# Both operand sums of a weight pair made together: gate/up by seven products in a two-layer decoder trunk

## The chip, the cores and the metric

The kernel runs on one core of one Trainium2 chip. The metric is the device time of that core in microseconds (us). Before the change three timed runs gave 2051.58, 2051.83 and 2052.47 us, a median of 2051.83 us. One further execution was taken by the profiler; every duration below comes from it. TensorE is called PE, VectorE DVE, ScalarE ACT, GpSimd POOL; SP is the engine that issues most of the weight loads.

## The reference

Two layers; each is a half-step feed-forward block (FFN), a mixer (a gated linear recurrence beside a sliding-window attention, both behind one wide projection) and a second half-step FFN. Width D = 1024, 512 tokens, inner FFN width 2816, everything in float32.

```
def swiglu(h, w_gate, w_up, w_down):
    return (jax.nn.silu(h @ w_gate) * (h @ w_up)) @ w_down

for l in range(DEPTH):
    h = rms_norm(x, gn[0])
    x = x + 0.5 * rms_norm(swiglu(h, w_ffn1_gate[l], w_ffn1_up[l], w_ffn1_down[l]), gn[1])
    h = rms_norm(x, gn[2])
    ...
    mixed = jax.nn.sigmoid(gate_a) * y_hg + jax.nn.sigmoid(gate_b) * y_at
    x = x + rms_norm(mixed @ w_out[l], gn[3])
    h = rms_norm(x, gn[4])
    x = x + 0.5 * rms_norm(swiglu(h, w_ffn2_gate[l], w_ffn2_up[l], w_ffn2_down[l]), gn[5])
```

## The kernel before

**Two halves of every operand.** Each float32 operand of a matmul is split into a high half (a cast, by ACT) and a low half (value minus high half), and a product is three matmuls: high by high, high by low, low by high (`mm3`). The weights stream from memory in units of 128x1024 float32 (`w32`, four buffers, loaded by SP at L244 and L247), and each unit is split into `whi` and `wlo` (six buffers of each). L359 is the cast to `whi` on ACT. The low half is made in one of two ways: by a subtraction on DVE (L363), or by writing the negated value on ACT (L355) and letting a POOL-issued DMA add the weight to it in memory (L358).

**Seven products.** Most gate and up columns are not computed as two plain products. A block of 128 gate columns, 128 up columns and the two halves of the 1024 input rows form a 2x2 block product that is computed with seven half-size products instead of eight (`sevenths`). For the weights this takes four operands per pair of units, the items a, b, c and d: a is the first unit `w`, d the second half of the second unit `v`, b is a tile `tt` of two sums of `w` and `v` (L340, L341), and c a second tile `tt` of two more sums, which start from b's first sum. a and d get their low halves through POOL's DMA, b and c through DVE's L363. One pair is 7 x 4 x 3 = 84 matmuls of 128x256. PE uses the pair in the order a (products 1 and 2), b (5 and 7), c (6 and 4), d (3).

**Loops.** `fast` runs such pairs: 15 of them in the first FFN and 19 in each of the three others, 72 together. The mixers' branch gates take 4 more pairs in each layer (`gates`), each followed by 24 matmuls of 128x512. So there are 80 pairs. Each loop starts with one short extra matmul of 144 columns (`lead`). After a `fast` loop comes `down`, which begins with three plain stretches (`both`) and then further seven-product work for the down projection, whose operands (`Late`) DVE, ACT and POOL make from the gated results.

**What a pair asks of DVE besides.** After the products of pair k DVE combines the PSUM results with L1063, L1065, L1069 and L1070, ACT applies the Silu (L1084), and DVE multiplies gate by up (L1087), the gated product.

**What sets the order.** Only PE follows the program as it is written. For the other engines a scheduler chooses, but instructions that go through `pin` (or `hold`, while `tight` is set in `fast`) keep the written order among themselves. `ahead` decides when the next item is split: up to four items ahead of the one that PE is using in `fast`, and no more than six items in flight. So item b of pair k+2 is split (and writes over the buffers of item d of pair k) while PE is in pair k+1, and c of pair k+2 when a of pair k+1 is free. The gated product is held back as `gate` and put out at a chosen place by `product()`, here within the split of b.

In numbers of the profile, b's and c's lines before the change are L340, L341 (sums of b), L359 and L363 (its halves), L347, L348 (sums of c), L359 and L363 again. A `tt` tile has two buffers.

Of the kernel before, what the change touches and what calls it, by code (L numbers as in the profile page):

```python
# [7 lines left out]
F32 = mybir.dt.float32  # L8
# [3 lines left out]
ALU = mybir.AluOpType  # L12
# [3 lines left out]
P = 128  # L16
D = 1024
# [29 lines left out]
def trunk(ctx: ExitStack, tc: tile.TileContext, xin, wall, gains, lbT, hgain, sinks, c_dist, c_mask, c_ident, out):  # L47
    nc = tc.nc
    cp = ctx.enter_context(tc.tile_pool(name="cp", bufs=1))
    sb = ctx.enter_context(tc.tile_pool(name="sb", bufs=1))  # L50
# [9 lines left out]
    def nm(s):  # L60
        seq[0] += 1
        return f"{s}_{seq[0]}"
# [85 lines left out]
    pin = tc.keep_in_program_order  # L148
# [10 lines left out]
    class Stream:  # L159
# [164 lines left out]
        def split(self):  # L324
            it = self.items[self.done]
            if it.kind[0] == "p":
                return self.quarter(it)
            u, last = it.u, it.kind in "uvd"
            self.load(u + (1 if it.kind in "uv" else 2))
            it.hi, it.lo = (sb.tile([P, D + 64], F32R, tag=t, name=nm(t), bufs=WS)[:, it.at : it.at + D] for t in ("whi", "wlo"))  # L330
            w, h = self.raw[u], (slice(0, D // 2), slice(D // 2, D))
            cols = (slice(0, D),)
            if it.kind == "u" and u < 2:
                cols = h
            if it.kind in "bcd":
                v = self.raw[u + 1]
            if it.kind == "b":

                self.t13 = sb.tile([P, D], F32, tag="tt", name=nm("tt"), bufs=2)
                pin(nc.vector.tensor_tensor(self.t13[:, h[0]], w[:, h[0]], v[:, h[0]], op=ALU.add))  # L340
                pin(nc.vector.tensor_tensor(self.t13[:, h[1]], v[:, h[0]], v[:, h[1]], op=ALU.add))  # L341
                w = self.t13
                self.product()
            elif it.kind == "c":

                t = sb.tile([P, D], F32, tag="tt", name=nm("tt"), bufs=2)
                pin(nc.vector.tensor_tensor(t[:, h[0]], self.t13[:, h[0]], v[:, h[1]], op=ALU.add))  # L347
                pin(nc.vector.tensor_tensor(t[:, h[1]], t[:, h[0]], w[:, h[1]], op=ALU.add))  # L348
                w = t
            elif it.kind == "d":  # L350
                w = v
                cols = h[1:]
            for c in cols:
                if it.kind in "vad":
                    i = nc.scalar.mul(it.lo[:, c], w[:, c], -1.0)  # L355
                    if self.pinned or self.tight:
                        pin(i)
                    nc.gpsimd.dma_start(it.lo[:, c].bitcast(F32), w[:, c], accum_op=ALU.add)  # L358
                i = nc.scalar.copy(it.hi[:, c], w[:, c])  # L359
                if u < 6 or self.pinned or self.tight:  # L360
                    pin(i)
                if it.kind not in "vad":
                    self.hold(nc.vector.tensor_tensor(it.lo[:, c], w[:, c], it.hi[:, c].bitcast(F32), op=ALU.subtract))  # L363
            self.done += 1
            self.flight += 1
            if last:
                nu = u + (1 if it.kind in "uv" else 2)
                for i in range(u, nu):
                    self.raw.pop(i)
                    self.freed += 1  # L370
                self.load(self.freed + W32)
# [128 lines left out]
    def pair_split(v, how=split):  # L500
        return how(v, to=(big(F32R, [P, 2, S // 2]), big(F32R, [P, 2, S // 2])))
# [13 lines left out]
    class First(Quarters):  # L515
# [44 lines left out]
        def sums(self):  # L560

            k = len(self.x56)
            a = []
            for i in range(2):
                f = xs[k + 4 * i]
                nc.vector.scalar_tensor_tensor(f, f, g_sb[:, 0, 0, k + 4 * i : k + 4 * i + 1], self.rb, op0=ALU.mult, op1=ALU.mult)
                a.append([f[:, c] for c in HALF])
            self.x124.append([])
            for v in (a[0][0], a[1][0], a[1][1]):
                x = big(F32R, [P, 2, S // 2])  # L570
                split(v, to=(x[:, 0, :], x[:, 1, :]))
                self.x124[k].append(x)
            for x, v in zip((self.x56, self.x37), quarter_sums(a[0][0], a[1][0], a[0][1], a[1][1])):
                x.append(pair_split(v))
# [74 lines left out]
    class Late:  # L649
# [20 lines left out]
        def first(self, k):  # L670
            x = big(F32R, [P, 2, S // 2])
            self.x1.append(split(self.src[k][:, HALF[0]], to=(x[:, 0, :], x[:, 1, :]), hold=pin))
# [979 lines left out]
```

## Time and profile before

| | |
|---|---|
| timed runs | 2051.58, 2051.83, 2052.47 us |
| the profiled execution, span | 2051.3 us |
| PE clock granted, mean | 0.999 |
| ACT's cast of a `tt` tile (L359, 128x1024) | 160 of 1051 ns (median) |
| DVE's low half of a `tt` tile (L363, 128x1024) | 160 of 1226 ns |
| a sum of 128x512 on DVE (L340, L341, L347, L348) | 80 each, 681 to 692 ns |
| ACT waiting for L348 before L359 | 192.3 us in 75 waits |
| DVE waiting for L359 before a `tt` tile's L363 | 129.1 us in 146 waits |

The span runs from the first to the last instruction of the profiled execution; the median of the timed runs is 0.5 us longer. Durations include a tail in which the next instruction of the same engine already runs: a matmul of 128x256 is listed with 0.28 us and the next one starts 0.113 us later, and a DVE instruction listed with 0.69 us is followed by the next after about 0.60. So lengths of stages are read from start to start. Idle time of an engine that nobody waits for costs nothing.

### The profile page before, as it was taken

Reading aid. Unit: us, or ns where it says so; the run is one execution under the profiler, and the core shown is the slowest. Engines: PE = TensorE matmul, PEld = TensorE weight load, DVE = VectorE, ACT = ScalarE, POOL = GpSimd, SP = SyncE. Lnnn points to the kernel's source line nnn. Section 1 sums busy time; section 2 is a strip of 40 time slices with the busy share of each in tenths; the row PEclk is TensorE's granted clock in tenths of the full one; section 3 lists DMA queues with packets and bytes.
Section 4 is the critical chain, followed back from the end, with each engine's and each line's share of the span. In section 5 each row is a group of like instructions: output and inputs, shape, how many; then the busy total and the mean of one; then the engine's idle time right before and its main releaser. Section 6 shows DMA issues by size and latency. Waiting matters only on the chain. (4 is left out here: it accounts for less than half of the span.)

```text
span 2051.3 us, 36423 instructions
## 1 busy us (share of the span) xinstructions
PE 2032.0 (99%) x13553; PEld 1815.3 (88%) x13553; DVE 1623.7 (79%) x2894; ACT 1249.4 (61%) x2213; POOL 268.3 (13%) x318
## 2 busy tenths in 40 slices
PE   9999999999999999999999999999999999999998
PEld 8899878877888999997899998888778989999987
DVE  5887889767676778888988878987686858788888
ACT  7556687446355556657866566874554545665684
POOL 0111140000000011113201111400000100111140
PEclk9999999999999999999999999999999999999999
DMA  8577788312237357778757778872122553777694
GB/s 257 152 194 186 189 187 238 117 65 70 73 94 215 113 146 192 190 188 205 200 157 191 193 186 203 179 230 92 62 73 62 137 194 102 182 190 194 175 201 123
DMA packets 166801, 328.07 MB, mean 160 GB/s; under 512 B 19072, under 2 KB 85088, under 8 KB 166624
## 3 DMA queue, kind: packets, MB, share of 16 engines
q1 hardware_dynamic: 122416, 228.16, 33.5%
q0 software_dynamic: 44064, 97.54, 27.3%
q8 instruction: 106, 1.74, 0.4%
q14 instruction: 71, 0.58, 0.1%
q10 hardware_dynamic: 144, 0.05, 0.0%
HBM read 213.43 MB, written 14.73 MB: 111 GB/s over the span
## 5 line engine op out<-in xcount | busy, mean ns | idle before, releaser
L116 PE MATMUL acc<-s,whi 128*128 128x256 f32 (+1 forms) x4998 | 1023.7, 304 | 0.3 <-ACT whi L359 0.3
L116 PEld LDWEIGHTS acc<-s,whi 128*128 128x128 f32 x4998 | 793.6, 188 | 47.0 <-issue 3.2
L116 PE MATMUL acc<-s,wlo 128*128 128x256 f32 (+1 forms) x2488 | 755.3, 304 | 5.3 <-DMA wlo<-w 5.2
L116 PEld LDWEIGHTS acc<-s,wlo 128*128 128x128 f32 x2488 | 467.9, 188 | 30.6 <-DMA wlo<-w 7.4
L116 PE MATMUL acc<-whi,s 128*128 128x512 f32 x1360 | 443.9, 394 | 4.9 <-ACT whi L288 3.6
L359 ACT CAST whi<-w 128x1024 fp32r<-128x1024 f32 (+1 forms) x310 | 284.8, 926 | 144.9 <-PE acc L116 103.5
L359 ACT CAST whi<-tt 128x1024 fp32r<-128x1024 f32 x160 | 168.1, 1051 | 250.5 <-DVE tt L348 192.3
L358 POOL DMA_DIRECT2D wlo<-w x178 | 154.7, 870 | 1232.8 <-ACT wlo L355 987.0
L116 PEld LDWEIGHTS acc<-whi,s 128*128 128x128 f32 x1360 | 255.8, 188 | 64.3 <-ACT whi L288 4.8
L363 DVE TENSOR_TENSOR wlo<-tt,whi 128x1024 fp32r<-128x1024 f32 x160 | 196.1, 1225 | 131.4 <-ACT whi L359 129.1
L116 PE MATMUL acc<-wlo,s 128*128 128x512 f32 x680 | 267.3, 393 | 1.8 <-DVE wlo L296 1.6
L116 PE MATMUL aux<-s,whi 128*128 128x256 f32 (+1 forms) x1296 | 228.5, 279 | 0.0
L363 DVE TENSOR_TENSOR wlo<-w,whi 128x1024 fp32r<-128x1024 f32 (+1 forms) x132 | 157.4, 1206 | 74.2 <-ACT whi L359 73.9
L116 PEld LDWEIGHTS aux<-s,whi 128*128 128x128 f32 x1296 | 196.6, 188 | 1.1 <-issue 0.5
L116 PE MATMUL aux<-s,wlo 128*128 128x256 f32 (+1 forms) x648 | 180.4, 278 | 0.0
L116 PEld LDWEIGHTS acc<-wlo,s 128*128 128x128 f32 x680 | 128.2, 188 | 32.1 <-DVE wlo L296 7.5
L355 ACT ACTIVATE wlo<-w 128x1024 fp32r<-128x1024 f32 (+1 forms) x178 | 153.1, 862 | 2.6 <-DMA w<-wall 1.9
L116 PE MATMUL aux<-whi,s 128*128 128x512 f32 x432 | 143.9, 390 | 0.0
L444 POOL DMA_DIRECT2D s<-s x128 | 111.1, 972 | 219.1 <-ACT s L432 100.2
L116 PEld LDWEIGHTS aux<-s,wlo 128*128 128x128 f32 x648 | 121.7, 188 | 0.3
L296 DVE TENSOR_TENSOR wlo<-s,whi 128x512 fp32r<-128x512 f32 x160 | 102.7, 686 | 9.9 <-ACT whi L288 8.1
L432 ACT CAST s<-s 128x512 fp32r<-128x512 f32 (+1 forms) x140 | 70.8, 548 | 44.8 <-DVE s L491 39.3
(184 smaller groups left out, 2466.9 us busy)
## 6 DMA issues: line engine op xcount, KB each, us to landing
w<-wall SPq DMA_DIRECT2D x267, 512.0 KB, 3.7
wlo<-w POOLq DMA_DIRECT2D x98, 512.0 KB, 5.1
w<-wall SPq DMA_DIRECT2D x224, 128.0 KB, 3.5
wlo<-w POOLq DMA_DIRECT2D x80, 256.0 KB, 3.3
s<-wall SPq DMA_DIRECT2D x128, 128.0 KB, 4.3
s<-s POOLq DMA_DIRECT2D x64, 256.0 KB, 5.0
x_d<-s SPq DMA_DIRECT2D x48, 256.0 KB, 4.6
s<-x_d SPq DMA_DIRECT2D x48, 256.0 KB, 5.1
```

The source lines that it names most:

```text
L116: nc.tensor.matmul(o, lhsT, rhs, start=start, stop=stop)
L296: pin(nc.vector.tensor_tensor(it.lo[:, h[c]], w[c], it.hi[:, h[c]].bitcast(F32), op=ALU.subtract))
L355: i = nc.scalar.mul(it.lo[:, c], w[:, c], -1.0)
L358: nc.gpsimd.dma_start(it.lo[:, c].bitcast(F32), w[:, c], accum_op=ALU.add)
L359: i = nc.scalar.copy(it.hi[:, c], w[:, c])
L363: self.hold(nc.vector.tensor_tensor(it.lo[:, c], w[:, c], it.hi[:, c].bitcast(F32), op=ALU.subtract))
L432: (hold or ws.hold)(nc.scalar.copy(hi, src))
L444: nc.gpsimd.dma_start(lo.bitcast(F32), src, accum_op=ALU.add)
```

## The change

Within the split of b all four sums are now formed. The second `tt` tile is allocated there and kept as `self.t`; its first half follows b's two sums at once, then comes the gated product, then its second half. The split of c finds its sums ready. No instruction is added or removed on any engine.

```
                 pin(nc.vector.tensor_tensor(self.t13[:, h[0]], w[:, h[0]], v[:, h[0]], op=ALU.add))
                 pin(nc.vector.tensor_tensor(self.t13[:, h[1]], v[:, h[0]], v[:, h[1]], op=ALU.add))
+                self.t = t = sb.tile([P, D], F32, tag="tt", name=nm("tt"), bufs=2)
+                pin(nc.vector.tensor_tensor(t[:, h[0]], self.t13[:, h[0]], v[:, h[1]], op=ALU.add))
+                self.product()
+                pin(nc.vector.tensor_tensor(t[:, h[1]], t[:, h[0]], w[:, h[1]], op=ALU.add))
                 w = self.t13
-                self.product()
             elif it.kind == "c":
 
-                t = sb.tile([P, D], F32, tag="tt", name=nm("tt"), bufs=2)
-                pin(nc.vector.tensor_tensor(t[:, h[0]], self.t13[:, h[0]], v[:, h[1]], op=ALU.add))
-                pin(nc.vector.tensor_tensor(t[:, h[1]], t[:, h[0]], w[:, h[1]], op=ALU.add))
-                w = t
+                w = self.t
```

In the changed program L343 and L345 are the two sums that were L347 and L348. On DVE one pair in the middle of the first loop reads as follows; `m`, `s` and `acc` are the combined results of the pair before, `tt_1430` is b's tile and `wlo_1429` its low half, `wlo_1462` (now `wlo_1465`) is c's low half.

```order
 L340 TENSOR_TENSOR tt_1430<-w_236_1243,w_237_1245 128x512
 L341 TENSOR_TENSOR tt_1430<-w_237_1245 128x512
+L343 TENSOR_TENSOR tt_1433<-tt_1430,w_237_1245 128x512
 L1087 SCALAR_TENSOR_TENSOR s_1417<-m_1383 128x512
+L345 TENSOR_TENSOR tt_1433<-tt_1433,w_236_1243 128x512
 L363 TENSOR_TENSOR wlo_1429<-tt_1430,whi_1428 128x1024
-L347 TENSOR_TENSOR tt_1463<-tt_1430,w_237_1245 128x512
-L348 TENSOR_TENSOR tt_1463<-tt_1463,w_236_1243 128x512
-L363 TENSOR_TENSOR wlo_1462<-tt_1463,whi_1461 128x1024
+L363 TENSOR_TENSOR wlo_1465<-tt_1433,whi_1464 128x1024
 L1063 TENSOR_TENSOR m_1510<-acc_1420,s_1423 128x2x256
```

Both sums of c have moved in front of b's low half, so that the two low halves stand one behind the other.

At the start of the second loop (the second FFN of layer 0), where fewer instructions are pinned, ACT's order changes more. The casts L432 there belong to the operands of the first pair made from the block's input, `whi_7810` is b's high half, `wlo_7782` a's negated weight, and L1106 the Silu that frees PSUM buffers of the plain products ahead of the loop. Before:

```order
L355 ACTIVATE wlo_7782<-w_1360_7491 128x1024
L432 CAST s_7875<-s_7869 128x512
L432 CAST s_7879<-s_7870 128x512
L359 CAST whi_7810<-tt_7812 128x1024
L432 CAST s_7893<-s_7887 128x512
L432 CAST s_7897<-s_7888 128x512
L1106 ACT_TABLE_LOAD
L1106 ACTIVATE s_7901<-acc_7607 128x512
L1106 ACTIVATE s_7905<-acc_7609 128x512
```

In the changed program the same stretch of ACT's order, with `whi_7931` as c's high half and `whi_7935`, `wlo_7936` as d's two, reads:

```order
L355 ACTIVATE wlo_7782<-w_1360_7491 128x1024
L359 CAST whi_7810<-tt_7812 128x1024
L432 CAST s_7878<-s_7872 128x512
L432 CAST s_7882<-s_7873 128x512
L359 CAST whi_7931<-tt_7815 128x1024
L359 CAST whi_7935<-w_1389_7568 128x512
L355 ACTIVATE wlo_7936<-w_1389_7568 128x512
L432 CAST s_7896<-s_7890 128x512
L432 CAST s_7900<-s_7891 128x512
L1106 ACT_TABLE_LOAD
L1106 ACTIVATE s_7904<-acc_7607 128x512
L1106 ACTIVATE s_7908<-acc_7609 128x512
```

The casts of c and d of the first pair have moved ahead of the Silu that frees `acc_7607`.

At the first gate pair of layer 0's mixer, `whi_6429` (now `whi_6432`) is c's high half, `whi_6463` and `wlo_6464` are d's, `wlo_6517` is a's of the next pair, L1051 copies the first product of the pair out of PSUM, and L1439 applies the gate of the branch before. ACT's order before:

```order
L432 CAST s_6375<-aux_6370 128x512
L432 CAST s_6399<-s_6393 128x512
L432 CAST s_6403<-s_6394 128x512
L432 CAST s_6419<-aux_6414 128x512
L1439 ACTIVATE s_6448<-acc_6407 128x512
L1051 COPY s_6479<-acc_6475 128x256
L359 CAST whi_6429<-tt_6431 128x1024
L359 CAST whi_6463<-w_1083_6087 128x512
L355 ACTIVATE wlo_6464<-w_1083_6087 128x512
L359 CAST whi_6485<-w_1096_6157 128x1024
L359 CAST whi_6516<-w_1118_6239 128x1024
L355 ACTIVATE wlo_6517<-w_1118_6239 128x1024
```

And with the change:

```order
L432 CAST s_6378<-aux_6373 128x512
L359 CAST whi_6432<-tt_6362 128x1024
L359 CAST whi_6463<-w_1083_6087 128x512
L359 CAST whi_6485<-w_1096_6157 128x1024
L355 ACTIVATE wlo_6464<-w_1083_6087 128x512
L359 CAST whi_6516<-w_1118_6239 128x1024
L432 CAST s_6402<-s_6396 128x512
L355 ACTIVATE wlo_6517<-w_1118_6239 128x1024
L432 CAST s_6406<-s_6397 128x512
L359 CAST whi_6545<-tt_6547 128x1024
L432 CAST s_6422<-aux_6417 128x512
L1439 ACTIVATE s_6448<-acc_6410 128x512
```

c's and d's casts and the next a's negated weight now stand ahead of the copy L1051 and of L1439, and two operand casts (`s_6402`, `s_6406`) stand behind the next a's high half. POOL's order is the same in both programs, and SP's differs in one load of a weight tile in each FFN, which now stands ahead of the load of a row of gains.

## The prediction

> **What bounds the kernel now.** I read the page first, then PE's waits, then one pair of the seven-product loop on DVE, ACT and PE, and last the start and end of each loop on PE.
>
> ```profile
> span 2051.3 us, 36423 instructions
> PE 2032.0 (99%) x13553; PEld 1815.3 (88%) x13553; DVE 1623.7 (79%) x2894; ACT 1249.4 (61%) x2213; POOL 268.3 (13%) x318
> PE acc L116 <- DMA wlo<-w: 5.2, 8, 1.2
> PEld acc L116 <- DMA wlo<-w: 7.4, 11, 1.4
> ```
>
> PE is the bound. Its only large named wait is for `wlo<-w`, the low halves of a and d that come through POOL's DMA. The 99% hides lost time, since a listed matmul reaches beyond the start of the next; so I go by starts. One pair in the middle of the first loop, DVE's rows and then PE's (start, length, engine, line, operation; in brackets the idle time before and what ended it):
>
> ```profile
> 195.51 0.68 DVE L1063 TENSOR_TENSOR m<-acc,s 128x512 f32<-128x512 f32 x1
> ...
> 200.35 1.23 DVE L363 TENSOR_TENSOR wlo<-tt,whi 128x1024 fp32r<-128x1024 f32 x1 [0.57 <-ACT whi L359]
> 201.49 0.68 DVE L347 TENSOR_TENSOR tt<-tt,w 128x512 f32<-128x512 f32 x1
> 202.21 0.69 DVE L348 TENSOR_TENSOR tt<-tt,w 128x512 f32<-128x512 f32 x1
> 204.07 1.23 DVE L363 TENSOR_TENSOR wlo<-tt,whi 128x1024 fp32r<-128x1024 f32 x1 [1.17 <-ACT whi L359]
> 205.22 0.68 DVE L1063 TENSOR_TENSOR m<-acc,s 128x512 f32<-128x512 f32 x1
> ```
> ```profile
> 190.32 0.28 PE L116 MATMUL aux<-s,whi 128*128 128x256 f32 x1
> 199.84 0.28 PE L116 MATMUL aux<-s,whi 128*128 128x256 f32 x1
> ```
>
> DVE's period is 205.22 - 195.51 = 9.71 us, PE's 199.84 - 190.32 = 9.52. DVE is not full: it idles 0.57 + 1.17 = 1.74 us of its period, each time for ACT's cast, because sums, cast and low half stand in one serial chain. So DVE falls 0.19 us further behind PE with each pair. That reaches PE through ACT's queue:
>
> ```profile
> 202.99 1.05 ACT L359 CAST whi<-tt 128x1024 fp32r<-128x1024 f32 x1 [2.40 <-DVE tt L348]
> 204.99 1.05 ACT L355 ACTIVATE wlo<-w 128x1024 fp32r<-128x1024 f32 x1
> 206.33 0.86 POOL L358 DMA_DIRECT2D wlo<-w  x1 [0.61 <-ACT wlo L355]
> ```
> ```profile
> DMA to landing us min/median/max: 3.2/4.8/6.1
> ```
>
> ACT waits 2.40 us for L348, and behind that cast stand the negated weights of d and of the next a, and POOL's DMA. The last line is that DMA's landing in the second loop. The pair to which this a belongs begins on PE at about 212.1 (199.84 + 9.53 is the next such `aux` row, and 24 matmuls of 0.113 lie between it and the pair's start), so the a has 212.1 - 206.3 = 5.8 us to land, and 0.19 us less with each pair. Against landings up to 6.1 PE must sooner or later wait.
>
> **The loops, counted.** Each loop from its short lead matmul to the first matmul of `down`, in program order:
>
> ```profile
> 88.20 0.51 PE L116 MATMUL acc<-s,whi 128*128 128x144 f32 x3
> 231.12 0.40 PE L116 MATMUL acc<-whi,s 128*128 128x512 f32 x1
> 728.74 0.51 PE L116 MATMUL acc<-s,whi 128*128 128x144 f32 x3
> 913.55 0.40 PE L116 MATMUL acc<-whi,s 128*128 128x512 f32 x1
> 1062.97 0.51 PE L116 MATMUL acc<-s,whi 128*128 128x144 f32 x3
> 1246.28 0.40 PE L116 MATMUL acc<-whi,s 128*128 128x512 f32 x1
> 1742.11 0.39 PE L116 MATMUL acc<-s,whi 128*128 128x144 f32 x2
> 1929.76 0.40 PE L116 MATMUL acc<-whi,s 128*128 128x512 f32 x1
> ```
>
> The first takes 142.92 us for 15 pairs, 9.528 each: no loss. At that rate 19 pairs take 181.03; the others take 184.81, 183.31 and 187.65, so they lose 3.78, 2.28 and 6.62, together **12.7 us**. The fourth is of another kind:
>
> ```profile
> 1771.60 0.39 PE L116 MATMUL acc<-s,wlo 128*128 128x256 f32 x1 [0.41 <-DMA wlo<-w]
> 1907.15 0.40 PE L116 MATMUL aux<-s,whi 128*128 128x256 f32 x2
> 1917.04 0.40 PE L116 MATMUL aux<-s,whi 128*128 128x256 f32 x2
> ```
>
> It waits once, early, and from there its pair takes 1917.04 - 1907.15 = 9.89 us at an unchanged clock: 84 matmuls 4.4 ns slower each. I read this as a second rhythm of PE into which a wait can throw it, and which holds to the end of the loop; the other loops came out of their waits in the quick one. Without the wait the 6.6 us go as well.
>
> **Behind the loops.** The same lag is paid once more in `down`. PE's first 168 matmuls there end at the first rows below, after loops one to four; the last gated product L1087 of each loop follows:
>
> ```profile
> 273.20 0.39 PE L116 MATMUL acc<-whi,s 128*128 128x512 f32 x1
> 954.71 0.39 PE L116 MATMUL acc<-whi,s 128*128 128x512 f32 x1
> 1288.92 0.39 PE L116 MATMUL acc<-whi,s 128*128 128x512 f32 x1
> 1968.04 0.39 PE L116 MATMUL acc<-whi,s 128*128 128x512 f32 x1
> ```
> ```profile
> 239.53 0.69 DVE L1087 SCALAR_TENSOR_TENSOR s<-m 128x512 f32<-128x512 f32 x1 [0.76 <-ACT m L1084]
> 921.05 0.69 DVE L1087 SCALAR_TENSOR_TENSOR s<-m 128x512 f32<-128x512 f32 x1 [0.76 <-ACT m L1084]
> 1255.26 0.69 DVE L1087 SCALAR_TENSOR_TENSOR s<-m 128x512 f32<-128x512 f32 x1 [0.76 <-ACT m L1084]
> 1934.37 0.69 DVE L1087 SCALAR_TENSOR_TENSOR s<-m 128x512 f32<-128x512 f32 x1 [0.76 <-ACT m L1084]
> ```
>
> The stretch takes 42.08, 41.16, 42.64 and 38.28 us. L1087 comes 8.41, 7.50, 8.98 and 4.61 us after the loop's last matmul. The difference of the two is 33.67, 33.66, 33.66 and 33.67: in all four the stretch ends a fixed time after L1087, so DVE's chain (operands of the down projection) sets it. In the fourth, where PE ran at 9.89 and DVE kept up, PE hardly waits: 168 matmuls at 0.227 are 38.1. Below a lag of about 4.4 us PE sets the end. Over the fourth the others lose 3.80 + 2.88 + 4.36 = **11.0 us**. Part of the third is a slower clock behind its longest wait, in 1272 to 1279 us:
>
> ```profile
> 1272.00:1279.00 7.00, 5.72 (x17) 4.29 (x18) 5.27 (x12) 4.60 (x10) 1.72 (x2) 0.76 1.02 251
> ```
>
> The granted clock is 0.76 there, worth about 0.24 x 7 = 1.7 us. The Trainium skill, "TensorE: Matmul & The Clock Gate", "What's actually happening", has PE drop to half its clock after an idle window of about 3.4 us. PE's starts lie only 1271.0 to 1273.0 apart there, so the row speaks against that figure. By the page the drop would not be owed to this wait and would stay: the gain would be 1.7 us less.
>
> **The change, part by part.** No instruction comes or goes; 80 pairs get another order. (1) L343 and L345 run where DVE stood still for b's cast, and when b's low half ends, c's cast has long begun. DVE's chain drops from 9.71 towards its filled time, 9.71 - 1.74 = 7.97 us, so PE's 9.52 sets the pace. (2) The gated product stands one sum later (0.6 us); nobody in the loop waits for it. b's low half too is later by at most the two sums, 1.2 us less the 0.57 that was idle; PE needs it only after a's two products (24 x 0.113 = 2.7 us into the pair), and b is made a pair ahead. (3) New waits: c's cast can now come before PE has freed its buffer (a of the pair before, 2.7 us into the pair). Queued behind it on ACT are d and the next a. Their buffers come free 5.4 and 8.2 us into the pair, so a goes to POOL at about 9.3 and has 19.05 - 9.3 = 9.7 us to land, against 6.1. (4) At the loops' end DVE goes from the last but one L1070 to the last L1087 in 12.1 us (from this row to 921.05):
>
> ```profile
> 908.94 0.68 DVE L1070 TENSOR_TENSOR m<-aux,s 128x512 f32<-128x512 f32 x1
> ```
>
> That L1070 can now start 0.1 to 2.4 us into the last pair (1.4 by my count, with a row weight's low half ahead of it), so the lag becomes 12.1 + 1.4 - 9.5 = 4.0, between 2.7 and 5.0. At 4.0 nothing of the 11.0 stays; at 5.0 some 0.4 in each of three stretches over the fourth. (5) Gates: the first layer's second pair waits for a's low half,
>
> ```profile
> 603.11 0.38 PE L116 MATMUL acc<-s,wlo 128*128 128x256 f32 x1 [1.22 <-DMA wlo<-w]
> ```
>
> and its negated weight now stands ahead of L1051: **1.2 us** gained, between 0 and 1.5. (6) Loop starts: the casts of c and d now stand ahead of the Silu that frees the buffer of the up product.
>
> ```profile
> 719.24 1.09 ACT L1106 ACTIVATE s<-acc 128x512 f32<-128x512 f32 x2
> 723.30 0.39 PE L116 MATMUL acc<-s,whi 128*128 128x512 f32 x1
> ```
>
> d's cast waits until PE has left the block before (717.8); with d's two halves (1.1), two casts (1.1) and the table load (1.3) the Silu comes at about 722, PE needs it by 723. I take 0, with a loss of up to 1.5 in each of three loops. SP's moved load waits for a weight buffer that now frees earlier: 0.
>
> The sum: 12.7 + 11.0 + 1.2 = 24.9 off the span, 2051.3 - 24.9 = 2026.4; the median lies 0.5 above the span, so **2027 us**.
>
> **Rivals.** *One loop falls into the slow rhythm* all the same: 19 x 0.365 = 6.9 more, 2034. For it: one of three loops with waits did so. Against: it came from a wait, and waits go. *The stretches behind the loops keep their loss*, because a load and not L1087 is the start of the fixed time: 2027 + 11 = 2038. Against: the fixed time fits to 0.01 us. *The change doesn't free the chain*, since c's cast finds another wait on ACT in the same place and DVE's period stays near 9.7: 2050 to 2052. Against: neither L1051 (1.4 us into the pair) nor the freed buffer (2.7) comes late enough. *Slower:* the slow rhythm from the start, by another alignment behind the lead matmul. In all 80 pairs it costs 80 x 0.365 = 29 us: 2056; it passes the old time only from about 70 pairs on. Against: all four loops started quick.
>
> **How the numbers follow.** The forecast (2023 to 2031) has 0.67, one slow loop 0.11, the lasting loss behind the loops 0.10, no relief 0.07, all slow 0.03, lower than 2023 0.02. The range takes the first three, 2023 to 2039. About 0.2% (4.1 us) can be told from no change here. Faster by more: 0.90; within: 0.07; slower: 0.03.
>
> **What would show it.** L363 of c without idle time before it, ACT's wait for the second sum gone from 192.3 us, each loop at 9.52 us a pair, L1087 at most 4.6 us behind the last matmul, no clock row below 0.9 near the third loop's end. A pair of 9.89, a named wait on `wlo` within the loops, or the 33.7 us still counting from L1087 with PE waiting would make it wrong.

## The result, and the profile after

| | before | after |
|---|---|---|
| timed runs, median (lowest to highest) | 2052.15 us (2051.58 to 2052.83) | 2024.78 us (2024.19 to 2025.95) |
| ratio after to before, 95% interval | | 0.9869 (0.9855 to 0.9883) |
| the profiled execution, span | 2051.3 us | 2022.4 us |
| loops one to four, lead to `down` | 142.92, 184.81, 183.31, 187.65 us | 142.92, 181.00, 181.00, 181.00 us |
| the 168 matmuls behind each loop | 42.07, 41.16, 42.65, 38.28 us | 38.11 us, four times |
| last L1087 behind the loop's last matmul | 8.41, 7.50, 8.98, 4.61 us | 3.92 or 3.93 us, four times |

The three lower rows are counted from starts, as in the prediction. The change makes the kernel 27.4 us faster by the medians, 28.9 by the two spans. The page of the changed kernel, its busy times and the two groups that the change is about; in a group's line the last part is the idle time before its instructions and what ended most of it:

```profile
span 2022.4 us, 36427 instructions
PE 2015.8 (100%) x13553; PEld 1808.9 (89%) x13553; DVE 1624.0 (80%) x2894; ACT 1264.7 (63%) x2213; POOL 268.3 (13%) x318
...
L359 ACT CAST whi<-tt 128x1024 fp32r<-128x1024 f32 x160 | 168.4, 1053 | 83.8 <-DVE tt L341 41.9
L363 DVE TENSOR_TENSOR wlo<-tt,whi 128x1024 fp32r<-128x1024 f32 x160 | 195.4, 1221 | 12.1 <-ACT whi L359 9.5
```

DVE does the same work in the same time (1624.0 us against 1623.7). What went is its standing still ahead of the low halves: 12.1 us against 131.4. No wait for `wlo<-w` is left among PE's waits, which now read (total, count, longest):

```profile
PE aux L116 <- DVE eps_t L139: 1.1, 1, 1.1
PE acc L126 <- DVE s L863: 1.0, 2, 0.5
```

The same pair in the middle of the first loop, DVE's rows, then ACT's and POOL's, then PE's:

```profile
195.20 0.69 DVE L343 TENSOR_TENSOR tt<-tt,w 128x512 f32<-128x512 f32 x1
195.80 0.69 DVE L1087 SCALAR_TENSOR_TENSOR s<-m 128x512 f32<-128x512 f32 x1
196.41 0.69 DVE L345 TENSOR_TENSOR tt<-tt,w 128x512 f32<-128x512 f32 x1
197.01 2.48 DVE L363 TENSOR_TENSOR wlo<-tt,whi 128x1024 fp32r<-128x1024 f32 x2
200.19 0.69 DVE L1063 TENSOR_TENSOR m<-acc,s 128x512 f32<-128x512 f32 x1 [0.70 <-PE acc L116]
...
202.91 0.69 DVE L1070 TENSOR_TENSOR m<-aux,s 128x512 f32<-128x512 f32 x1 [0.84 <-PE aux L116]
```
```profile
201.55 1.06 ACT L355 ACTIVATE wlo<-w 128x1024 fp32r<-128x1024 f32 x1 [1.58 <-PE aux L116]
...
202.91 0.86 POOL L358 DMA_DIRECT2D wlo<-w  x1 [2.29 <-ACT wlo L355]
```
```profile
212.23 0.39 PE L116 MATMUL acc<-s,whi 128*128 128x256 f32 x2
```

Both low halves (x2) run in one piece. DVE now waits only for PE, 0.70 and 0.84 us in a pair, and ACT's negation of the next a waits for PE too. ACT still waits for c's second sum (now L345), 31.7 us in 65 waits, the longest 0.8, where it was 192.3 in 75. PE waits for nobody. The DMA for the pair that begins at 212.23 is issued at 202.91 instead of 206.33, 9.3 us ahead.

The start of loops three and four, their end, the last row of the stretch behind each, and the last L1087:

```profile
1049.20 0.51 PE L116 MATMUL acc<-s,whi 128*128 128x144 f32 x3
1230.20 0.40 PE L116 MATMUL acc<-whi,s 128*128 128x512 f32 x1
1268.30 0.39 PE L116 MATMUL acc<-whi,s 128*128 128x512 f32 x1
1720.71 0.51 PE L116 MATMUL acc<-s,whi 128*128 128x144 f32 x3
1901.71 0.40 PE L116 MATMUL acc<-whi,s 128*128 128x512 f32 x1
1939.82 0.39 PE L116 MATMUL acc<-whi,s 128*128 128x512 f32 x1
```
```profile
1222.01 0.68 DVE L1070 TENSOR_TENSOR m<-aux,s 128x512 f32<-128x512 f32 x1
1234.12 0.69 DVE L1087 SCALAR_TENSOR_TENSOR s<-m 128x512 f32<-128x512 f32 x1 [0.76 <-ACT m L1084]
1905.64 0.69 DVE L1087 SCALAR_TENSOR_TENSOR s<-m 128x512 f32<-128x512 f32 x1 [0.76 <-ACT m L1084]
```

1230.20 - 1049.20 and 1901.71 - 1720.71 are both 181.00, the figure without any loss; 1268.30 - 1230.20 and 1939.82 - 1901.71 are both 38.11 (to the rounding of the rows). The stretch of the windows view that answers to the slow clock near the third loop's end (time, busy times and counts of the engines, granted clock, DMA share, GB/s):

```profile
1251.00:1258.00 7.00, 7.00 (x33) 5.79 (x32) 5.27 (x12) 4.61 (x10) 1.72 (x2) 1.00 1.08 259
```

DVE, ACT and POOL have the same 12, 10 and 2 instructions in it as before; PE has 33 matmuls in it instead of 17, at a granted clock of 1.00 where it was 0.76. This wait of PE, the longest there, stood ahead of the slow clock before:

```profile
1272.97 0.50 PE L116 MATMUL acc<-whi,s 128*128 128x512 f32 x1 [1.59 <-ACT whi L288]
```

### The profile page after: what moved, and what is told of

Same layout as the page of the kernel before. It is cut to its first block, busy times and chain, and to the rows that moved or that the text cites. A ratio compares the mean times of both kernels' runs of the same rounds, so it can differ in the third digit from the quotient of the medians.

```text
span 2022.4 us, 36427 instructions
## 1 busy us (share of the span) xinstructions
PE 2015.8 (100%) x13553; PEld 1808.9 (89%) x13553; DVE 1624.0 (80%) x2894; ACT 1264.7 (63%) x2213; POOL 268.3 (13%) x318
## 4 chain that ended last, share of the span: by engine, by line
PE 96%; DVE 2%; ACT 1%; issue 0%; DMA 0%; SPq 0%; DVEq 0%; ACTq 0%
PE acc L116 73%; PE aux L116 21%; PE aux L126 2%; DVE wlo L296 1%; PE acc L126 0%; DMA w<-wall 0%; DVE s L264 0%; DVE wlo L363 0%; DVE s L968 0%; ACT s L442 0%; ACT whi L288 0%; DVE s L863 0%; ACT s L443 0%; ACT whi L359 0%; DVE s L433 0%
## 5 line engine op out<-in xcount | busy, mean ns | idle before, releaser
L363 DVE TENSOR_TENSOR wlo<-tt,whi 128x1024 fp32r<-128x1024 f32 x160 | 195.4, 1221 | 12.1 <-ACT whi L359 9.5
L296 DVE TENSOR_TENSOR wlo<-s,whi 128x512 fp32r<-128x512 f32 x160 | 102.7, 685 | 9.9 <-ACT whi L288 9.9
L1070 DVE TENSOR_TENSOR m<-aux,s 128x512 f32<-128x512 f32 x80 | 55.2, 690 | 52.0 <-PE aux L116 51.5
```

Source lines behind the costliest of these rows:

```text
L296: pin(nc.vector.tensor_tensor(it.lo[:, h[c]], w[c], it.hi[:, h[c]].bitcast(F32), op=ALU.subtract))
L1070: ws.hold(nc.vector.tensor_tensor(m[:, 1:3, :], pairs[2], v[:, ::-1, :], op=ALU.add))
```

## The experiments

All variants start from the changed kernel. In their rows lines behind an inserted one are a few numbers higher than in the changed kernel; the names say which they are. The theory throughout: PE's 9.52 us a pair is the floor, and all that matters is whether DVE's chain per pair is below it.

### What of the change counts: the product's place, one sum, both sums

Edit one puts the gated product where it was, ahead of both sums of c:

```
+                self.product()
                 self.t = t = sb.tile(...)
                 pin(... t[:, h[0]] ...)
-                self.product()
                 pin(... t[:, h[1]] ...)
```

> The gated product stands ahead of both sums of c, as in the kernel before; only the sums are early. My theory (what counts is that both sums and the cast of c no longer stand between b's low half and c's): DVE's period stays under PE's 9.52 us, so the loops stay at 142.9 and 181.0 us, the stretches behind them at 38.1, and the time at that of the changed kernel, 2024 to 2026 us. Rival (the new place of the product between the sums is part of the gain, because it delays the results that fill PE's queue less or more): a lag of the last L1087 other than 3.9 us, and the time above 2028.

Edit two leaves the second sum in the split of c:

```
                 pin(... t[:, h[0]] ...)
                 self.product()
-                pin(... t[:, h[1]] ...)
...
             elif it.kind == "c":
+                pin(... self.t[:, h[1]] ...)
```

> Only c's first sum is made in b's split; the second stays in c's, behind b's low half, so c's cast still waits for it. My theory (DVE needs only 0.19 us of its 1.74 us idle per pair to get below PE's 9.52): the first idle gap (0.57 us) is filled, DVE's period is 9.1 to 9.2 us, the loops run at 9.52 and nearly all of the gain is there, 2024 to 2028 us; the lag of the last L1087 may be up to 1 us longer than 3.9, worth at most 0.6 us in each stretch. Rival (the gain needs c's cast to run beside b's low half, that is both sums early): DVE stays near 9.6 to 9.7, waits for the low halves return, 2035 to 2050 us.

Measured: 2025.12 us (2024.88 to 2025.35; ratio to before 0.9867, 0.985 to 0.9883) and 2025.51 us (2024.54 to 2026.35; 0.9868, 0.9854 to 0.9883). Neither can be told from the changed kernel. In both the loops take 142.92 and 181.00 us, and the lag of the last L1087 is 3.9 (4.2 behind the second loop with one sum early, where the stretch takes 38.11 all the same). With one sum early, DVE in the first half of the second loop:

```profile
783.18 0.68 DVE L1087 SCALAR_TENSOR_TENSOR s<-m 128x512 f32<-128x512 f32 x1
783.83 1.23 DVE L363 TENSOR_TENSOR wlo<-tt,whi 128x1024 fp32r<-128x1024 f32 x1
784.97 0.69 DVE L348 TENSOR_TENSOR tt<-tt,w 128x512 f32<-128x512 f32 x1
786.83 1.23 DVE L363 TENSOR_TENSOR wlo<-tt,whi 128x1024 fp32r<-128x1024 f32 x1 [1.17 <-ACT whi L359]
```

The idle time of 0.57 ahead of b's low half is gone and the 1.17 ahead of c's is still there. From L1063 to L1063 DVE takes 8.98 us while it catches up, then 9.52. So the product's place is worth nothing, and half of the change is as good as the whole: 9.71 had to come below 9.52, and 8.98 does.

### How much room is left: more work on DVE

```
                 pin(... t[:, h[0]] ...)
+                for _ in range(2):
+                    pin(... t[:, h[0]] ...)
                 self.product()
```

> The changed kernel with c's first sum computed three times instead of once (the same values written again): 2 x 0.6 = 1.2 us more on DVE in each of the 80 pairs. My theory (PE's 9.52 us sets the pace as long as DVE's chain is below it): DVE's period is 8.0 + 1.2 = 9.2 us, so nothing is lost in the loops: 2024 to 2029 us, with up to 1 us more lag behind each loop. Rival (the gain is proportional to DVE's time in the pair): 80 x 1.2 = 96 us less half or more of it hidden, above 2045 us.

The same with `range(4)`:

> The same sum computed five times: 4 x 0.6 = 2.4 us more on DVE in each pair. My theory: DVE's period is 8.0 + 2.4 = 10.4 us, above PE's 9.52, so it sets the pace once the head start is used up: 0.9 us for each of some 50 to 76 pairs and 3 to 5 us behind each loop, 2075 to 2115 us, and L1063 to L1063 takes 10.4 us late in the loops. Rival (the idle time of DVE that is left can still absorb it): below 2040 us.

Measured: 2025.21 us (2024.85 to 2025.95; 0.9868, 0.9853 to 0.9883) with two more, 2121.58 us (2121.36 to 2122.34; 1.0338, 1.0322 to 1.0353) with four. The first is as forecast: L1063 comes every 9.24 us early in loops two to four and every 9.52 late, and nothing is lost. The second is above the range given. Its DVE in the second loop, its loop's end, the last gated product (L1089 there) and the end of the stretch behind:

```profile
886.23 0.68 DVE L343 TENSOR_TENSOR tt<-tt,w 128x512 f32<-128x512 f32 x1
886.95 2.87 DVE L345 TENSOR_TENSOR tt<-tt,w 128x512 f32<-128x512 f32 x4
889.74 0.69 DVE L1089 SCALAR_TENSOR_TENSOR s<-m 128x512 f32<-128x512 f32 x1
```
```profile
943.50 0.40 PE L116 MATMUL acc<-whi,s 128*128 128x512 f32 x1
951.01 0.69 DVE L1089 SCALAR_TENSOR_TENSOR s<-m 128x512 f32<-128x512 f32 x1 [0.76 <-ACT m L1086]
984.62 0.39 PE L116 MATMUL acc<-whi,s 128*128 128x512 f32 x1
```

The five sums take 889.74 - 886.23 = 3.51 us; with 0.60 for the last, ahead of L1089, each repetition costs 0.73, not the 0.60 that I had taken. DVE's period is 10.69, and PE follows it: the four loops take 156.3, 203.6, 203.8 and 203.4 us, 81.1 more than in the changed kernel. Behind the loops the old loss is back: the lag is 951.01 - 943.50 = 7.51, and the stretch ends 984.62 - 951.01 = 33.61 us after the product (33.59 to 33.64 after all four). The four stretches are 12.3 us longer. Between 9.24 and 10.69 lies the bend, where the theory puts it.

### One loss or two: the new order in the last four pairs only

```
+                    it.new = (i >= n - 4) if n > 1 else False
...
+                if it.new:
                     self.t = t = sb.tile(...)
...
             elif it.kind == "c":
+                if not it.new:
+                    ...
                 w = self.t
```

> The new order in the last four pairs of each of the four loops only, the old order in the other pairs and in the gates. My theory (two separate losses: PE waits inside the loops once the lag has grown, and the lag left at the end delays the stretch behind): four pairs at a DVE period of 8.0 take back 4 x 1.5 = 6 us of lag, so the stretches behind loops come to 38.1 to 38.6 us and the loops keep most of their loss (9 to 13 of the 12.8 us), gates keep 1.5: 2036 to 2042 us. Rival (one loss, not two: the lag is made good by PE's waits, and what is won behind is lost within): within 2 us of either of the two kernels.

Measured: 2039.58 us (2038.5 to 2040.58; 0.9937, 0.9922 to 0.9952), as the first theory has it. The stretches behind the loops are at 38.11, all four. The loops take 142.92, 185.29, 186.92 and 183.98 us: 13.2 us of loss, a little over the 9 to 13 expected, and the second gate pair takes 1.4 us too long in the first layer and 0.35 in the second. So the waits inside the loops and the lag at their end are two bills from the same cause, and four pairs at the end pay the second. In the last pairs DVE runs free, at 7.79 us a pair.

Two of these loops went into the slow rhythm of 9.89 us a pair. The third, the start of three pairs' `aux` products and the wait between the first two:

```profile
1109.59 0.39 PE L116 MATMUL aux<-s,whi 128*128 128x256 f32 x2
1113.50 0.38 PE L116 MATMUL acc<-s,wlo 128*128 128x256 f32 x1 [0.80 <-DMA wlo<-w]
1120.44 0.40 PE L116 MATMUL aux<-s,whi 128*128 128x256 f32 x2
1130.33 0.40 PE L116 MATMUL aux<-s,whi 128*128 128x256 f32 x2
```

Ahead of the wait the pairs take 9.52, behind it 1130.33 - 1120.44 = 9.89, to the loop's end, though the last pairs wait for nothing. Some 13 pairs of this loop and 6 or 7 of the second are slow, at 0.37 us each: about 7 of the 13.2 us are this rhythm, and the rest is waiting.

### The gates: the new order in the loops only

```
+                    it.new = (True) if n > 1 else False
```

> The new order in the 72 pairs of the four loops, the old one in the 8 pairs of the mixers' gates. My theory: the gates give 1.5 us of the gain (first layer's second pair back at about 11.1 instead of 9.64 us) and perhaps the rest that I had not placed (1.1 us ahead of the first gate): 2025 to 2028 us. Rival (the gates are no part of it): the time of the changed kernel within 0.5 us.

Measured: 2025.39 us (2024.78 to 2026.01; 0.9868, 0.9853 to 0.9883): the difference from the changed kernel is too small to tell the two apart, and the time lies in the theory's range as well, so the profile has to decide. In it the second gate pair of the first layer takes 9.64 us from lead to end, without a wait, although the gates have the old order; with the same order in the kernel of four last pairs it takes 11.0. The low half that the pair waits for is a's; its DMA is issued in the old order (before, and in this kernel, where L366 is the same line) and in the new at

```profile
593.46 0.86 POOL L358 DMA_DIRECT2D wlo<-w  x1 [1.99 <-PE acc L116]
```
```profile
589.01 0.86 POOL L366 DMA_DIRECT2D wlo<-w  x1 [1.99 <-PE acc L116]
```
```profile
584.17 0.86 POOL L358 DMA_DIRECT2D wlo<-w  x1 [5.56 <-ACT wlo L355]
```

The first gate's lead stands at 586.27, 581.81 and 581.37 us, so the DMA goes out 7.2 us behind it in both kernels with the old order and 2.8 in the new. The last number of these rows of the DMA view is its landing:

```profile
wlo<-w POOLq DMA_DIRECT2D x1, 512.0 KB, 9.6
```
```profile
wlo<-w POOLq DMA_DIRECT2D x1, 512.0 KB, 8.0
```
```profile
wlo<-w POOLq DMA_DIRECT2D x1, 512.0 KB, 5.0
```

593.46 + 9.6 = 603.06 is where PE's wait of 1.22 us ended before; with 8.0 us it is in time. In the kernel of four last pairs, where PE waited, it took 9.4. In the old order the landing decides whether PE waits; in the new one the DMA goes out 4.4 us sooner, so that a landing of 9.6 would be in time too. So the 1.5 us at the gates are not a fixed price of the old order. What sets the landing time is open.

### The two rhythms of PE

Without the short matmul ahead of the pairs:

```
         if first:
-            lead(p1, w.hi[:, :P], pre.operand(1)[0][0], LEAD)
+            pass
```

> The changed kernel without the short extra matmul of 144 columns ahead of each chain of pairs (its result is overwritten in any case). My theory on the slow rhythm of the fourth loop before (9.89 instead of 9.52 us a pair at full clock): it is an alignment of PE's stream which the length of this matmul sets and a wait can upset; without it the loops fall into the slow rhythm, 0.37 us a pair: 15 to 29 us more, 2040 to 2054 us. Rival (the rhythm hangs on waits alone): the loops stay at 9.52, 2023 to 2026 us.

Measured: 2052.72 us (2051.91 to 2055.15; 1.0003, 0.9993 to 1.0013). The change's whole gain is gone, by this alone. Two pairs of the first loop:

```profile
154.95 0.40 PE L116 MATMUL aux<-s,whi 128*128 128x256 f32 x2
164.84 0.40 PE L116 MATMUL aux<-s,whi 128*128 128x256 f32 x2
```

Every pair of the four loops takes 9.89 us, at full clock and with no wait of PE beyond the two of the changed kernel: 117.7 ns a matmul instead of 113.3. Then one more short matmul in the middle of each loop:

```
+MID = (64, 96, 128, 160)
...
-            m = sevenths(pre, early, j == start)
+            m = sevenths(pre, early, LEAD if j == start else widths[-1] if j == start + 8 else 0)
```

> The changed kernel with one more short matmul ahead of the ninth pair of each loop, of 64, 96, 128 and 160 columns in loops one to four (its result is overwritten); it waits for nothing. Theory (alignment alone sets the rhythm): in some of the loops the pairs behind it take 9.89 us, 7 x 0.37 = 2.6 us in the first and 11 x 0.37 = 4.0 us in each other loop so hit, and which loops depends on the width: 2026 to 2038 us. Rival (only a wait upsets the rhythm): all pairs at 9.52 and four times 0.03 to 0.07 us more, 2024 to 2026 us.

Measured: 2040.81 us (2039.63 to 2041.14; 0.9942, 0.9928 to 0.9957), over the upper end: it is not some loops that change but all four. The fourth, pairs eight to ten by their `aux` rows, with the short matmul between the first two:

```profile
1807.29 0.39 PE L117 MATMUL aux<-s,whi 128*128 128x256 f32 x2
1810.01 0.51 PE L117 MATMUL acc<-s,whi 128*128 128x160 f32 x3
1817.18 0.28 PE L117 MATMUL aux<-s,whi 128*128 128x256 f32 x1
1827.08 0.40 PE L117 MATMUL aux<-s,whi 128*128 128x256 f32 x2
```

The loops take 2.73 and three times 4.22 us longer. No wait is needed, then; a short matmul does it. Which ones do was asked with other widths:

```
+MID, SECOND = ((256,), (96, 96), (240,), (64, 64, 64)), ((), (144,), (64,), (112, 112), (240,))
...
-                        lead(o[j][:, c], blocks[k, j][2], pre.h[k][0][:, c], LEAD_IN)
+                        for n in quads[-1] if half else (LEAD_IN,):
+                            lead(o[j][:, c], blocks[k, j][2], pre.h[k][0][:, c], n)
```

> The changed kernel with other short matmuls, at two places; their results are overwritten. (1) Ahead of the ninth pair of loops one to four: one of 256 columns, two of 96, one of 240, three of 64. (2) In the five plain stretches done in two halves of 256 columns (two FFN starts of each kind and the mixers), the one of 112 columns in the second half, behind which the trace shows 117.7 ns a matmul, is replaced: none, 144, 64, two of 112, 240. Theory A (each matmul shorter than its neighbours moves PE to the other rhythm): loops one and two stay at 9.52 us a pair, three and four go to 9.89; in the second halves the first and the fourth stay at 117.7 ns and the rest do not follow from it, since 112 did not move it. Theory B (the count of matmuls decides, odd or even): loop one goes to 9.89, two stays, three and four go. Theory C (a phase in time decides, which some widths hit): the five second halves differ by width, some at 113.3 ns. Time: 2024 + 2.6 (loop one, if hit) + 4.0 for each other loop hit, less 0.4 for each second half made quick: 2030 to 2035 us by A, 2033 to 2037 by B.

Measured: 2037.53 us (2036.7 to 2039.58; 0.9929, 0.9907 to 0.9952), just above both ranges, since loops two, three and four took 4.2 to 4.4 us longer each, and only one half got quick. What each width did, this run and the others together:

| place | rhythm ahead of it | stays or comes out slow | stays or comes out quick |
|---|---|---|---|
| start of the loops | (none) | no short matmul | 144 |
| ninth pair | quick | 64, 96, 128, 160, two of 96, 240, three of 64 | 256 |
| first halves of the plain stretches (unchanged) | slow | | 112 |
| second halves of the plain stretches | slow | none, 112, 144, two of 112, 240 | 64 |

Theory A falls with the two of 96, theory B with these and with the 256. C, a phase in time, is left, and nothing here says what the phase is measured against; most widths stood at one place only. In the second halves, the short matmul and the first one behind the 90, for 64 columns (10.34 us) and for two of 112 (10.83):

```profile
1031.52 0.39 PE L117 MATMUL acc<-s,whi 128*128 128x64 f32 x2
1041.86 0.40 PE L117 MATMUL acc<-s,whi 128*128 128x512 f32 x1
...
1362.67 0.50 PE L117 MATMUL acc<-s,whi 128*128 128x112 f32 x3
1373.50 0.63 PE L117 MATMUL acc<-s,whi 128*128 128x512 f32 x2
```

### A version that follows from it

The changed kernel still ran its five second halves in the slow rhythm. One number changes that:

```
-                        lead(o[j][:, c], blocks[k, j][2], pre.h[k][0][:, c], LEAD_IN)
+                        lead(o[j][:, c], blocks[k, j][2], pre.h[k][0][:, c], 64 if half else LEAD_IN)
```

> The changed kernel with the short matmul of the second halves 64 columns wide instead of 112, all else as changed; its result is overwritten. By the third of the five second halves in the run before, the 90 matmuls behind it go from 118.5 to 114.5 ns: five times 0.36 = 1.8 us less, 2022.4 to 2023.6 us. Rival (the rhythm found there depends on what stood before it in that run): fewer than five of them quick, and less than 1 us.

> The changed kernel itself once more, beside the one with 64 columns on the same chip: 2024 to 2026 us; what differs between its profile and the first one at equal instructions is scatter. Of the 2.9 us that the change gave outside the loops, the stretches behind them and the gates, I expect this profile to take back about 1 to 2 us.

Measured on one chip: 2023.02 us (2022.45 to 2024.44; ratio to before 0.9858, 0.9844 to 0.9873) against 2024.94 us (2024.64 to 2025.13; 0.9866, 0.985 to 0.9883) for the changed kernel. The medians are 1.9 us apart and the two sets of runs do not overlap, though the intervals of the ratios do. The fifth half, with 64 and (in the first profile of the changed kernel) with 112 columns:

```profile
1699.38 0.39 PE L116 MATMUL acc<-s,whi 128*128 128x64 f32 x2
1709.71 0.63 PE L116 MATMUL acc<-s,whi 128*128 128x512 f32 x2
```
```profile
1699.09 0.51 PE L116 MATMUL acc<-s,whi 128*128 128x112 f32 x3
1709.80 0.39 PE L116 MATMUL acc<-s,whi 128*128 128x512 f32 x1
```

10.33 against 10.71 us, and the same in the other four halves: 114.5 ns a matmul behind the short one, where it was 118.5.

## Why the prediction was right

The forecast was 2027.0 us, the median is 2024.78; the span was forecast at 2026.4 and is 2022.4. Step by step:

- **The bound and the cause.** Right. DVE's 9.71 us a pair against PE's 9.52 was the cause: half of the new order is enough, 1.5 us more on DVE costs nothing, 2.9 us more cost 97 us.
- **The loops, 12.7 us.** 12.8 measured. Each pair takes 9.52 and the fourth loop stayed quick. A second rhythm into which a wait can throw PE showed again in two loops of the kernel with four late pairs, behind a wait each time; a short matmul alone does it too.
- **Behind the loops, 11.0 us.** 11.7 measured: right in mechanism, too small in size. I had taken the fourth stretch, 38.28, as the floor; the floor is 38.11, in all four. PE's named waits in the first three, for ACT's L288 and DVE's L296 and L433, came to 6.5 us before and are gone; the 5.2 us for `wlo<-w` were not the only large ones. The lag of 4.0 came out as 3.92, from an L1070 at 1.3 us into the last pair (1222.01 - 1049.20 = 172.81 behind the lead, where the last pair begins at 181.00 - 9.52 = 171.48; 1.4 was counted) and 12.1 us on to L1087. The fixed 33.67 us behind L1087 held at a lag of 7.5 us with 33.6. That two terms are to be added, and not one, is shown by the kernel of four late pairs.
- **The clock.** Of the third stretch 1.7 us were put down to a granted clock of 0.76 behind the longest wait. That was misread: with the drop the stretch ended 33.66 us behind L1087 as it did without one in the first two, so the slow clock cost nothing in it. It filled time in which PE would have waited: 3 and 8 us behind its longest wait PE waits again in the first stretch, for 0.69 and 0.31 us, and in the third it does not. With the wait of 1.59 us gone the row reads 1.00, and in none of the twelve profiles without it does the clock drop before the last 4 us; so the one drop came and went with that wait. A wait alone is not enough, for one of 1.45 us in the first stretch left the clock at 1.00, and so did waits of up to 1.7 us in the kernel with four more sums; what else it takes is not shown. By the rule of the Trainium skill, "TensorE: Matmul & The Clock Gate", "What's actually happening" (an idle window of about 3.4 us comes first), the drop would not have been owed to the wait, it would have stayed, and the gain would have been 1.7 us less. It did not stay. Before, the clock was 0.50 from 1274.1 to 1277.5 us and 1.00 on either side; that the window is about 3.4 us long, as the Trainium skill says in the same place, is not contradicted.
- **DVE's chain, 7.97 us.** 7.79 where it runs free. I had taken off the idle times as listed, which begin at the listed ends, 0.09 us behind the next possible start (0.69 against 0.60). Two of these are the 0.18. a's DMA was to have 9.7 us to land; it has 9.3. Neither decides. That ACT's wait for c's second sum would be gone was too much said: 31.7 of 192.3 us are left, and PE waits for none of it.
- **Gates, 1.2 us.** 1.5 in the profile. But of three profiles with the old order there one has no wait either, so the term was a chance of a late DMA and not a price.
- **Loop starts and SP, 0.** No difference at these places in the two profiles.
- **What the sum lacked.** 2.9 us of the 28.9 lie outside these places: late in each `down` and in the plain stretches behind it, in steps of 0.1 to 0.4 us. I did not see them. At four of them, about 6 us behind each stretch's end, every profile of the changed kernel and its near variants shows the same 0.11 to 0.12. The rest differs between executions: over the same places the second profile of the changed kernel is 1.9 us shorter than before (so about 1 us is scatter, as expected of it), and the kernel with old gates 1.6. What makes them up is open, and one profile of the kernel before cannot tell.
- **Span to time.** I had added 0.5 us, from before's median and span. In the four runs of the changed kernel the time lies 1.8 us above the span. By chance this took back 1.3 of the 4.0 by which the span was missed.

Of the rivals, the loss behind the loops going on, and the chain not freed, did not come. The slow rhythm in all pairs was priced at 29 us; brought about by leaving out the short matmul it costs 27.8 (2052.72 - 2024.94), just the old time.

## What to carry to other kernels

When a busy engine falls behind PE by 0.2 us a turn, look for idle time within its serial chain before moving work off it: interleaving the sums of two operands over the wait for the first one's cast was worth 1.3%, and half of it would have done. Count such a lag twice, where PE waits inside the loop and where the stage behind needs the last result; and once the period is below PE's, further relief is worth nothing. When short matmuls stand in a stream, look at the start-to-start time behind each of them: a width that suits one place is wrong at another.

## What was not expected of the hardware

- A stream of 128x256 matmuls has two steady speeds at full granted clock, 113.3 and 117.7 ns from start to start, 3.9% apart, and keeps the one it has until a wait or a matmul of another width comes. A whole loop of 19 pairs in the slow one costs 7 us (19 x 0.37). On a quick stream all seven insertions that were not of 256 columns turned it slow; on a slow one, 64 columns of five insertions at one place turned it quick, and 112 at another. The Trainium skill, "TensorE: Matmul & The Clock Gate", "Back-to-back issue gap", gives N / 2.4 + 2.5 ns as the isolated gap from one matmul to the next at full clock, by which 256 columns take 109.2 ns (an estimate from that formula of the Trainium skill); no stretch of 256-column matmuls here ran at that.
- A DVE sum that is repeated onto the same tile costs 0.73 us where sums with other tiles between cost 0.60. It need not be a repetition: before, L348 stood right behind L347, whose result it reads, and started 202.21 - 201.49 = 0.72 us after it.
